# Layer 1, from the mixing sub-layer to the MLP: other tiles for the first weight group, no weight split on GpSimd, token-block sums from whole float32 tokens

## The chip, the core and the metric

The kernel runs on one core of a Trainium2 chip. Its engines have instruction streams of their own: TensorE (PE) multiplies and transposes, VectorE (DVE) and ScalarE (ACT) do elementwise work, GpSimd (POOL) does some of it too, SyncE (SP) issues nearly all DMAs. The metric is the device time of one execution in microseconds (us). Three runs of the kernel before took 1518.51, 1513.12 and 1522.53 us.

## The reference

Two layers over 512 latent tokens and 256 context tokens, 1024 features, all in float32. What matters here is the end of a layer's mixing and its MLP:

```
y   = merge_heads(attn, sgu, four, g_mix, w_out)        # output projection
x   = x + g1 * rmsnorm(y, g_post_mix)
hx2 = rmsnorm(x, g_pre_ff) * (1.0 + sc2) + sh2          # modulated tokens
x   = x + g2 * rmsnorm(square(relu(hx2 @ w_ff1)) @ w_ff2, g_post_ff)
```

In the second layer (layer 1, the last one) only the latent tokens go through this.

## The kernel before, in words

**Numbers.** Every operand of a product is held in two float32r parts, a high part (a cast) and a low part (the float32 value less the high part), and a product is three matmuls: high by high, high by low, low by high. So each weight block that comes in as `raw` is cast to `hi` by ACT (L234) and `lo` is made by a subtraction on DVE or POOL (L235, in `wunit`); each modulated token chunk is written in float32 by ACT (L393, `xv`), its high part by POOL (L395), its low part by DVE (L396).

**The MLP of layer 1.** The 4096 hidden features are worked in 16 groups of 256. Groups 0 and 1 use the plain product (`ff1`, L1106) for token blocks 0 and 1 and then for 2 and 3, since those tokens come in two halves. From group 2 on, `wino` (L1182) uses Winograd's form of Strassen's product: seven products in place of eight, which want sums of token blocks, S1 to S4 (`wino_a`), and differences of weights. With v11, v12 the modulated features of token blocks 0 and 1 (first and second half of the features) and v21, v22 those of blocks 2 and 3: S1 = v21 + v22, S2 = S1 - v11, S3 = v11 - v21, S4 = v12 - S2. Before, `wino_a` adds them up again from the two parts: per pair of feature chunks four adds on DVE and three on POOL for S1 to S3, then one on DVE and two on POOL for S4 (L956), and each S is split by ACT (L952) and DVE (L953). There are two such pairs.

**Tiles.** A tag of a pool is a ring: who asks for a tile of the tag waits until the one that had the buffer has been read for the last time. `w` has 8 tiles for weights, `raw` 4, `E` 4 and `PT` 2 belong to the attention while it runs, `Ma` 4; `h1`, `h2`, `h3` have two temporaries each. `h1` serves the sums s1 (and, in the new code, s3) and also the rectified hidden features `r` (L1122). The hidden products `h...` sit in two PSUM banks (tag S) until ACT has read them into `r`. The transposed tokens `xT` (L379) sit in two other banks.

**Order.** A scheduler places the instructions of each engine in one fixed order by a timeline of its own, with earlier calls of the program first. At run time an engine works strictly down its list. So what matters is which row stands ahead of which.

**Names.** In the rows `h100x` is layer 1, hidden group 0, half 0 of its 256 features, latent tokens; `h110x` the same of group 1. `raw_f`, `hi_f`, `lo_f` are weights of the MLP, `po1x` the output projection, `Ma1x` the split attention output, `at1x` the same before the split, `xr1x` the residual, `y1x` its normalised tokens, `f11x` the two parts of the modulated tokens, `wt`, `w` the products of Winograd's form, `f210x` the second product of the MLP for group 0.

Of the kernel before, what the change touches and what calls it, by code (L numbers as in the profile page):

```python
# [11 lines left out]
F32 = mybir.dt.float32  # L12
F32R = mybir.dt.float32r
BF16 = mybir.dt.bfloat16
AF = mybir.ActivationFunctionType
ALU = mybir.AluOpType
AX = mybir.AxisListType.X

P = 128
D = 1024  # L20
KD = D // P
# [10 lines left out]
# How far the first product of the MLP goes ahead of other work.  # L32
HP = 5
# The engine (v or p) that takes each of the two-operand steps of a hidden group: low parts of the weights of the
# first and second product, differences of weights, low parts of the hidden features.
# [10 lines left out]
# What the tensor engine does beside the attention units of a layer: U, G, F load the weights of a column group  # L46
# of the in-projection and u, g, f project a token block with them, fc, fx step through the Fourier mixing,
# gc, gx load the gates, oc, ox step through the output projection, ada through a modulation.
# [13 lines left out]
def _bc(ap, n, axis):  # L62
    """ap with a broadcast dimension of n put in at free position `axis`."""
    v = ap.unsqueeze(axis)
    shape = list(v.shape)
    shape[axis] = n
    return v.to_broadcast(shape)
# [3 lines left out]
def kernel(ctx: ExitStack, tc: tile.TileContext, a: dict, out: bass.AP):  # L71
# [15 lines left out]
    # Temporaries of a chain come from h1, h2, h3 in this order, so that chains never wait in a circle.  # L87
# [9 lines left out]
    # Streams that run side by side have tiles of their own; within a tag tiles are handed out in program order.  # L97
# [35 lines left out]
    # ------------------------------------------------------------- constants  # L133
# [18 lines left out]
    def rows_in(name, width, pairs):  # L152
        """Rows at given partitions of a zeroed [32, width] tile."""
        t = act.tile([32, width], F32, name=name, tag="slot")
        nc.gpsimd.memset(t, 0.0)
        for r0, src in pairs:
            nc.sync.dma_start(t[r0:r0 + src.shape[0], :], src)
        return t

    def turned(t, name, use):  # L160
        """Feature-major pieces of four chunks of such rows in PSUM, handed to `use`."""
# [7 lines left out]
    # silu(c), silu(c_ctx) as two columns of a zero-padded stationary operand  # L169
# [37 lines left out]
    # ---------------------------------------------------- common small helpers  # L207
# [4 lines left out]
    def power(o, i, scale, bias, expo):  # L212
        """o = (i * scale + bias) ** expo"""
# [11 lines left out]
    def wunit(src, shape, name, lo_eng=None, part=None, hi_pool=False):  # L225
        """A weight unit in two float32r parts whose sum is the float32 weight."""
# [11 lines left out]
    # ------------------------------------------------------------------ adaLN  # L238
    # modc[l]: feature-major columns for (sh1, sc1, sh2, sc2); gates go to DRAM rows.
# [7 lines left out]
    def ada_quad(l, q, alloc, alloct, wtile, side=None):  # L247
        """A sixth of the modulation of a layer. side: the rows of the weight times their entries are summed over
        the row chunks beside the tensor engine, which is left with the sum over the partitions."""
# [73 lines left out]
    def ada_rest(steps, alloc, alloct, side=None):  # L323
        """Steps through (layer, quad), one row chunk of the weight at a time."""
        for l, q in steps:
            yield from ada_quad(l, q, alloc, alloct, wa, side)
# [6 lines left out]
    # ------------------------------------------------- feature-major activations  # L333
    class Feat:
        """Feature-major tokens in two float32r parts, eight chunks of 128 features: with a tile for
        every chunk (whole=True, wide moving operands) or tiles for every token block."""
# [20 lines left out]
        def dests(self, k2, b0):  # L357
            """Destinations (hi, lo, slice of the [128, 2, 256] source) for chunks 2 k2, 2 k2 + 1."""
# [23 lines left out]
    def modulate(xns, feat, b0, l, which, alloc, order=range(KD // 2)):  # L382
        """Normalised token blocks b0, b0 + 1 -> modulated, feature-major, in two parts."""
# [4 lines left out]
        for k2 in order:  # L388
            ps = transposed(xns, nm, k2, alloc)
            v = h2([P, 2, n], F32, f"xv{nm}{k2}")  # L390
# [3 lines left out]
            for hi, lo, i in feat.dests(k2, b0):  # L394
                nc.gpsimd.tensor_scalar(out=hi, in0=v[:, i], scalar1=1.0, scalar2=1.0, op0=ALU.mult, op1=ALU.mult)  # L395
                nc.vector.tensor_tensor(out=lo, in0=v[:, i], in1=hi.bitcast(F32), op=ALU.subtract)  # L396

    # ------------------------------------------------------------- projections
# [14 lines left out]
    def in_group(l, nm, c0, c1, feats, consume, alloc, alloc2, units=None):  # L413
        """Loads a column group of w_in; the function returned projects one token block. What `consume` puts
        into `later` comes behind the products of the next block."""
# [19 lines left out]
    def rotate(ps, rope, nh, which, b, name):  # L435
        """Rotary embedding of a token-major [128, nh * 64] block in PSUM."""
# [14 lines left out]
    # ------------------------------------------------------------------ layers  # L451
    feats0 = {"c": Feat("c", "f00", False), "x": Feat("x", "f00", False)}
    # The start: shift and scale come a quarter of the features at a time, and behind each quarter the products
    # of its features with columns 256 .. 768 of the in-projection for the token blocks that are there.
# [8 lines left out]
    def ada_quarter(f):  # L463
        """Columns f * 256 .. of shift and scale of layer 0; four row chunks at a time share the tensor engine."""
# [46 lines left out]
    def layer(l, feats):  # L511
# [15 lines left out]
        # ---- in-projection and what follows from each column group  # L527
# [43 lines left out]
        def got_q(j, kind, b, ps, alloc):  # L571
            """Heads 4 j .. 4 j + 3: rotated, scaled, high parts over low parts along the partitions."""
# [24 lines left out]
        def gelu2(ps, out_, name):  # L597
            """out_ = 2 gelu(ps), in the tanh form; returns the [128, 256] temporary it used."""
# [60 lines left out]
        def part1(kind, k, hl, t0, n):  # L659
            """Tokens t0 .. t0 + n of a chunk of the gating and Fourier features."""  # L660
# [4 lines left out]
        def finish_s(kind, msf, nb):  # L665
            """msf: [128, nb], the mean squares of the Fourier part (plus eps) of every block."""
# [19 lines left out]
        def fourier(kind):  # L686
            """Three steps, for other work to lie between them."""
# [41 lines left out]
            for j in range(2):  # L729
                g = gg[j]  # L730
                # P in columns 0 .. H, then Q from its second column on
# [27 lines left out]
        def att_scores(kind, b, j):  # L759
            """Softmax numerators of four heads and 1 / their sums, token-major: (head, key chunk) -> [128, 128]."""  # L760
# [14 lines left out]
            for g in (0, 2):  # L775
                # negated scores, the masked ones 1e30, leave PSUM with their running minimum
# [32 lines left out]
        def att_values(kind, b, j, lob, pieces, ri, rest):  # L809
# [17 lines left out]
            # 1 / sum of every head and token, spread over the partitions of the head  # L827
# [37 lines left out]
        def postnorm(kind, b, y, G, which, dest, pieces=HALVES):  # L865
            """x + gate * rmsnorm(y), stored where the next reader wants it."""
# [23 lines left out]
        def out_proj(kind, alloc, alloc2):  # L890
            """Steps through the output projection: first the part of the gating and Fourier features, then for
            every two token blocks that of the attention and, at the end, what follows from it."""
# [35 lines left out]
            for b0 in bs[::2]:  # L928
# [7 lines left out]
                modulate(xns, f2[kind], b0, l, 1, alloc2)  # L936
# [5 lines left out]

        def wino_a(k2, alloc, which):
            """The sums S1 .. S4 of token blocks in Winograd's form of Strassen's product, for two feature chunks."""
# [40 lines left out]
        def flow(us, order, jobs):  # L985
            """Attention units, the scores of one ahead of the values of the one before. Behind every unit come
            the steps of `jobs` that `order` names; the attention goes first where both could."""
# [426 lines left out]
```

## Time and profile before

| what | value |
|---|---|
| runs | 1518.51, 1513.12, 1522.53 us; median 1518.51 us |
| profiled execution | span 1516.8 us from first to last instruction; the profile gives no other time for it |
| PE busy | 1429.4 us, 94% of the span |
| DVE, ACT, POOL busy | 74%, 49%, 42% |
| mean granted TensorE clock | 0.985 of full speed |
| DMA | 177.58 MB, 117 GB/s in the mean |

The span and the median of the runs differ by 1.7 us. PE is busy nearly always, so the time is PE's work and PE's idle time; but a matmul that runs at half clock counts as busy too. To find what a stage loses, one takes the stretches of 10 us: PE's busy time, the granted clock in the column PEclk, and then the instruction before which PE stood idle, with the releaser that the profile names.

### The profile page before, as it was taken

Reading aid. Unit: us, or ns where it says so; the run is one execution under the profiler, and the core shown is the slowest. Engines: PE = TensorE matmul, PEld = TensorE weight load, DVE = VectorE, ACT = ScalarE, POOL = GpSimd, SP = SyncE. Lnnn points to the kernel's source line nnn. Section 1 sums busy time; section 2 is a strip of 40 time slices with the busy share of each in tenths; the row PEclk is TensorE's granted clock in tenths of the full one; section 3 lists DMA queues with packets and bytes.
Section 4 is the critical chain, followed back from the end, with each engine's and each line's share of the span. In section 5 each row is a group of like instructions: output and inputs, shape, how many; then the busy total and the mean of one; then the engine's idle time right before and its main releaser. Section 6 shows DMA issues by size and latency. Waiting matters only on the chain. (4 is left out here: it accounts for less than half of the span.)

```text
span 1516.8 us, 24509 instructions
## 1 busy us (share of the span) xinstructions
PE 1429.4 (94%) x9133; PEld 1252.7 (83%) x9133; DVE 1115.8 (74%) x2003; ACT 747.7 (49%) x1673; POOL 644.3 (42%) x608
## 2 busy tenths in 40 slices
PE   7999999999899999999989998999998899999997
PEld 4688798788788878888878887998777788989886
DVE  3366887858687877878777758788757987777685
ACT  3346666556534333343333445476656555554452
POOL 3212636646634333334433546234346644344241
PEclk9999999999999999999999999999998999999999
DMA  9634322435132332325554344213134133223322
GB/s 328 228 122 154 112 74 84 137 115 167 42 100 84 124 111 84 126 70 174 167 172 129 125 160 139 72 55 87 39 100 165 56 112 111 93 89 100 110 84 84
DMA packets 94352, 177.58 MB, mean 117 GB/s; under 512 B 5796, under 2 KB 59524, under 8 KB 94232
## 3 DMA queue, kind: packets, MB, share of 16 engines
q1 hardware_dynamic: 91224, 170.93, 35.0%
q0 software_dynamic: 3008, 5.08, 1.2%
q8 instruction: 72, 1.18, 0.3%
q14 instruction: 48, 0.39, 0.1%
HBM read 166.62 MB, written 9.46 MB: 116 GB/s over the span
## 5 line engine op out<-in xcount | busy, mean ns | idle before, releaser
L1152 POOL TENSOR_TENSOR raw_f<-raw_f,raw_f 128x512 f32<-128x512 f32 x70 | 98.2, 1402 | 107.8 <-DVE raw_f L1152 89.5
L1147 ACT CAST Wf<-raw_f 128x512 fp32r<-128x512 f32 x98 | 60.4, 619 | 118.6 <-DMA raw_f<-in_w_ff 108.4
L266 DVE SCALAR_TENSOR_TENSOR acc<-wa,silu,acc 128x1024 f32<-128x1024 f32 x70 | 96.1, 1391 | 21.7 <-DMA wa<-in_w_ada 21.6
L1148 POOL TENSOR_TENSOR Wf<-raw_f,Wf 128x512 fp32r<-128x512 f32 x28 | 40.1, 1433 | 153.3 <-ACT Wf L1147 153.3
L1195 PE MATMUL wc<-f01c,Wf 128*128 128x256 f32 x672 | 98.5, 286 | 3.4 <-DVE p L1201 3.4
L1195 PEld LDWEIGHTS wc<-f01c,Wf 128*128 128x128 f32 x672 | 91.6, 194 | 7.9 <-DVE p L1201 3.8
L1148 DVE TENSOR_TENSOR Wf<-raw_f,Wf 128x512 fp32r<-128x512 f32 x70 | 62.0, 887 | 41.0 <-ACT Wf L1147 40.9
L234 ACT CAST hi_f<-raw_f 128x1024 fp32r<-128x1024 f32 x72 | 73.8, 1043 | 34.8 <-PE f208c L1247 6.6
L235 POOL TENSOR_TENSOR lo_f<-raw_f,hi_f 128x1024 fp32r<-128x1024 f32 x20 | 54.7, 2735 | 77.7 <-ACT hi_f L234 57.6
L1125 DVE TENSOR_TENSOR hx<-r,hx 128x256 fp32r<-128x256 f32 x98 | 61.5, 630 | 31.2 <-ACT r L1124 31.1
L235 DVE TENSOR_TENSOR lo_f<-raw_f,hi_f 128x1024 fp32r<-128x1024 f32 x52 | 76.6, 1478 | 1.3 <-ACT hi_f L234 1.0
L1123 ACT ACTIVATE hx<-r 128x256 fp32r<-128x256 f32 x112 | 45.4, 413 | 44.4 <-PE f203x L1247 8.7
L1182 PE MATMUL w<-f11x,Wf 128*128 128x256 f32 x336 | 65.1, 283 | 0.0
L1182 PE MATMUL w<-S,Wf 128*128 128x256 f32 x336 | 63.0, 283 | 0.0
L1122 ACT ACTIVATE r<-c 128x256 f32<-128x256 f32 x84 | 34.7, 414 | 55.5 <-DVE c L1201 43.4
L1182 PEld LDWEIGHTS w<-f11x,Wf 128*128 128x128 f32 x336 | 54.7, 191 | 1.5
L1182 PEld LDWEIGHTS w<-S,Wf 128*128 128x128 f32 x336 | 53.0, 191 | 1.7 <-issue 0.4
L1182 PE MATMUL w<-f01x,Wf 128*128 128x256 f32 x336 | 50.4, 284 | 1.9 <-ACT Wf L1147 1.0
L1182 PEld LDWEIGHTS w<-f01x,Wf 128*128 128x128 f32 x336 | 46.4, 191 | 5.3 <-ACT Wf L1147 1.4
L1124 ACT ACTIVATE r<-r 128x256 f32<-128x256 f32 x112 | 45.5, 413 | 1.9
L393 ACT ACTIVATE xvx<-xTx,mod 128x256 f32<-128x256 f32 x64 | 31.6, 560 | 18.2 <-PE xTx L379 11.9
L797 ACT ACTIVATE E0x<-E0x,mx_0x 128x512 f32<-128x512 f32 (+1 forms) x32 | 24.9, 778 | 12.9 <-DVE mx_0x L791 12.7
(1243 smaller groups left out, 4886.1 us busy)
## 6 DMA issues: line engine op xcount, KB each, us to landing
raw_f<-in_w_ff SPq DMA_DIRECT2D x128, 512.0 KB
wa<-in_w_ada SPq DMA_DIRECT2D x80, 512.0 KB
wq<-in_w_ada SPq DMA_DIRECT2D x16, 512.0 KB
raw_out0c<-in_w_out SPq DMA_DIRECT2D x8, 512.0 KB
raw_out0x<-in_w_out SPq DMA_DIRECT2D x8, 512.0 KB
res0x<-xr0x SPq DMA_DIRECT2D x8, 512.0 KB
raw_out1x<-in_w_out SPq DMA_DIRECT2D x8, 512.0 KB
xl0x<-in_x SPq DMA_DIRECT2D x4, 512.0 KB
```

The lines of the kernel that those rows point to most:

```text
L234: nc.scalar.copy(hi, raw)
L235: (lo_eng or nc.vector).tensor_tensor(out=lo, in0=raw, in1=hi.bitcast(F32), op=ALU.subtract)
L266: nc.vector.scalar_tensor_tensor(out=acc[r], in0=w, scalar=s, in1=acc[r], op0=ALU.mult, op1=ALU.add)
L1122: nc.scalar.activation(r, src, AF.Relu)
L1123: nc.scalar.activation(hv[:, 0], r, AF.Square)
L1124: nc.scalar.activation(r, r, AF.Square)
L1125: next(lo_h).tensor_tensor(out=hv[:, 1], in0=r, in1=hv[:, 0].bitcast(F32), op=ALU.subtract)
L1147: nc.scalar.copy(t[:, 0], src)
L1148: next(lo).tensor_tensor(out=t[:, 1], in0=src, in1=t[:, 0].bitcast(F32), op=ALU.subtract)
L1152: next(diff).tensor_tensor(out=o, in0=x, in1=y, op=ALU.subtract)
L1182: nc.tensor.matmul(ps, W[w][:, wl, k], A[k // 2][:, k % 2, xh], start=(m == 0), stop=(m == 11))
L1195: nc.tensor.matmul(ps, W[f"{k // 4 + 1}{j + 1}"][:, wl, k % 4], f2["c"].ap(k, xh, 0, CTX), start=(m == 0), stop=(m == 3 * KD - 1))
```

## The change

Only layer 1 is touched (`last` in the code); layer 0 and all that comes before the last output projection stay as they are.

1. Hidden group 0: the split weights go to tiles of `PT` and `E`, which the attention has left, in place of `w`. Group 1's hidden features go to `w` in place of `E`.
2. The low parts of these weights are all made on DVE; before, the second half of each group was made on POOL.
3. `modulate` of the latent tokens goes through the feature chunk pairs in the order 0, 2, 1, 3 and keeps the float32 values of token blocks 0 and 1 in two slots (`vw`). For blocks 2 and 3 (`vl`) the sums S1 to S4 are made right there, from the float32 values: per pair three adds on DVE and one on POOL. `wino_a` is not called any more in this layer.

```diff
-    def modulate(xns, feat, b0, l, which, alloc, order=range(KD // 2)):
+    def modulate(xns, feat, b0, l, which, alloc, order=range(KD // 2), keep=None, after=None):
...
-            v = h2([P, 2, n], F32, f"xv{nm}{k2}")
+            v = keep(k2) if keep else h2([P, 2, n], F32, f"xv{nm}{k2}")
...
+            if after:
+                after(k2, v)
...
-                modulate(xns, f2[kind], b0, l, 1, alloc2)
+                if last:
+                    modulate(xns, f2[kind], b0, l, 1, alloc2, (0, 2, 1, 3), *(wino_keep if b0 == 0 else wino_sums))
+                else:
+                    modulate(xns, f2[kind], b0, l, 1, alloc2)
...
+        def keep_whole(k2):
+            if k2 % 2 == 0:
+                for k in (0, 2):
+                    if ("t", k) not in whole:
+                        whole["t", k] = slot([P, 2, 2, 2 * P], F32, f"vw{k}")
+            whole[0, k2] = whole["t", k2 // 2 * 2][:, k2 % 2]
+            return whole[0, k2]
+
+        def keep_last(k2):
+            whole[1, k2] = h2([P, 2, 2 * P], F32, f"vl{k2}")
+            return whole[1, k2]
+
+        def sums_at(k2, v):
+            if k2 < 2:
+                return
+            k2 -= 2
+            v11, v12, v21, v22 = (whole[i, k2 + j] for i in range(2) for j in (0, 2))
+
+            def part(i, f):
+                t = slot([P, 2, 2, 2 * P], F32R, f"S{l}{i}{k2}")
+                WS[i, k2] = t
+                nc.scalar.copy(t[:, :, 0], f)
+                nc.vector.tensor_tensor(out=t[:, :, 1], in0=f, in1=t[:, :, 0].bitcast(F32), op=ALU.subtract)
+
+            def made(al, i, x, y, op, eng=nc.vector):
+                t = al([P, 2, 2 * P], F32, f"s{i}{l}{k2}")
+                eng.tensor_tensor(out=t, in0=x, in1=y, op=op)
+                return t
+
+            s1 = made(h1, 1, v21, v22, ALU.add)
+            s2 = made(h3, 2, s1, v11, ALU.subtract)
+            part(1, s1)
+            part(2, s2)
+            part(3, made(h1, 3, v11, v21, ALU.subtract, nc.gpsimd))
+            part(4, made(h3, 4, v12, s2, ALU.subtract))
...
-                           .rearrange("(k p) f -> p k f", p=P), [P, 4, 256], f"f1{l}{g}{u}", nc.gpsimd if g < 2 and u else None) for u in range(2)]
+                           .rearrange("(k p) f -> p k f", p=P), [P, 4, 256], f"f1{l}{g}{u}",
+                           nc.gpsimd if u and not last else None, (ptile, etile)[u] if last and g == 0 else None)
+                     for u in range(2)]
...
-            H[g]["x"] = [etile([P, 2, SEQ], F32R, f"hx{l}{g}{j}") for j in range(2)]
+            H[g]["x"] = [(wtile if last and g else etile)([P, 2, SEQ], F32R, f"hx{l}{g}{j}") for j in range(2)]
...
-        for which in range(2):
+        for which in range(0 if last else 2):
```

How the rows move. First ACT, at the start of layer 1's MLP. Before, the rectified features `r100x` follow the last copies of the residual's chain, far ahead of the first S. Of the new list (`vl` are the float32 tokens of blocks 2 and 3, `S` the sums' high parts):

```order
L394 ACTIVATE vl_12612<-xTx_12607,mod_4141 128x256
L394 ACTIVATE vl_12622<-xTx_12617,mod_4141 128x256 [waits PE_49,Pool_49]
L974 CAST S_12594<-s_12589 128x2x256 [waits DVE_49]
L974 CAST S_12599<-s_12597 128x2x256
L974 CAST S_12604<-s_12602 128x2x256 [waits DVE_49]
L974 CAST S_12631<-s_12627 128x2x256 [waits DVE_49]
L974 CAST S_12634<-s_12629 128x2x256 [waits DVE_49]
L974 CAST S_12639<-s_12637 128x2x256 [waits Pool_49]
L1172 ACTIVATE r100x_12712<-h100x_12687 128x256 [waits DVE_49]
L1173 ACTIVATE hx_12659<-r100x_12712 128x256 [waits Activation_49]
```

`r100x`, which clears the PSUM bank of `h100x`, now stands behind seven of the eight S casts, and takes the `h1` tile that `s_12627` (S1 of the second pair) had.

PE at the same place, the new list: the transposes of token blocks 2 and 3 and the first product of hidden group 1.

```order
L379 MATMUL xTx_12607<-ident,y1x_12133 128x128 [waits PE_49,Activation_49]
L379 MATMUL xTx_12607<-ident,y1x_12148 128x128
L379 MATMUL xTx_12617<-ident,y1x_12133 128x128 [waits PE_49,Activation_49]
L379 MATMUL xTx_12617<-ident,y1x_12148 128x128
L1156 MATMUL h110x_12747<-f11x_12313,hi_f_12663 128x256 [waits Activation_49]
L1156 MATMUL h110x_12747<-f11x_12313,hi_f_12663 128x256
```

Before, `h110x` followed `h101x` at once, and these transposes came 35 to 70 rows later, between the products of group 1 and of the second half. Now nothing but transposes lies between `h101x` and `h110x`.

DVE at the end of the output projection, the list before:

```order
L914 SCALAR_TENSOR_TENSOR y1x_12133<-po1x_12479,ra_1x_12107,y1x_12133 128x512
L882 SCALAR_TENSOR_TENSOR xr1x_12401<-y1x_12011,rp_1x_12411,xr1x_12401 128x512
L656 SCALAR_TENSOR_TENSOR Ma1x_12126<-at1x_12221,cols,Ma1x_12126 128x128 x2
L235 TENSOR_TENSOR lo_f_12612<-raw_f_12609,hi_f_12611 128x1024
```

and the new one:

```order
L917 SCALAR_TENSOR_TENSOR y1x_12133<-po1x_12477,ra_1x_12107,y1x_12133 128x512
L885 SCALAR_TENSOR_TENSOR xr1x_12401<-y1x_12011,rp_1x_12411,xr1x_12401 128x512
L235 TENSOR_TENSOR lo_f_12664<-raw_f_12661,hi_f_12663 128x1024
L885 SCALAR_TENSOR_TENSOR xr1x_12401<-y1x_12011,rp_1x_12411,xr1x_12401 128x512
L235 TENSOR_TENSOR lo_f_12670<-raw_f_12667,hi_f_12669 128x1024
L659 SCALAR_TENSOR_TENSOR Ma1x_12126<-at1x_12221,cols,Ma1x_12126 128x128 x2
```

All six weight splits of groups 0 and 1 and of the second product now stand on DVE ahead of the low part of the last attention unit (`Ma1x` from `at1x_12221`, L656, now L659); before, none of them did.

## Rows read from the trace of the kernel before

**Rows 1.** Stretches: length, busy PE, PEld, DVE, ACT, POOL (count), PEclk, DMA share, GB/s.
```profile
1140.00:1150.00 10.00, 6.35 (x29) 5.55 (x29) 10.00 (x11) 7.42 (x13) 8.12 (x8) 0.66 0.63 215
...
1190.00:1200.00 10.00, 4.94 (x20) 3.89 (x19) 9.96 (x10) 5.64 (x9) 7.05 (x5) 0.75 0.00 0
1200.00:1210.00 10.00, 10.00 (x64) 9.31 (x64) 10.00 (x15) 3.75 (x8) 3.78 (x3) 0.91 0.35 107
```
**Rows 2.** Timeline of PE: start, length, line, tiles, idle before and releaser.
```profile
1136.40 0.62 PE L909 MATMUL po1x<-hi_out1x,Ma1x 128*128 128x512 f32 x2
1137.92 0.38 PE L851 MATMUL ar1x<-unit,at1x 128*128 128x1 f32 x2 [0.89 <-POOL at1x L847]
...
1141.29 1.75 PE L379 MATMUL xTx<-ident,y1x 128*128 128x128 f32 x7 [2.82 <-DVE y1x L370]
...
1151.02 0.58 PE L1106 MATMUL h100x<-f11x,hi_f 128*128 128x256 f32 x1 [3.12 <-DVE f11x L396]
...
1156.98 0.50 PE L1106 MATMUL h110x<-f11x,hi_f 128*128 128x256 f32 x2
...
1168.16 0.60 PE L379 MATMUL xTx<-ident,y1x 128*128 128x128 f32 x4
...
1189.88 0.28 PE L1182 MATMUL wt<-S,Wf112t 128*128 128x256 f32 x1
1191.41 0.39 PE L1182 MATMUL wt<-S,Wf112t 128*128 128x256 f32 x1 [1.25 <-ACT S L952]
1194.72 1.40 PE L1182 MATMUL wt<-S,Wf112t 128*128 128x256 f32 x6 [2.92 <-DVE S L953]
1197.01 1.44 PE L1182 MATMUL wt<-S,Wf112t 128*128 128x256 f32 x5 [0.89 <-DVE S L953]
...
1201.87 0.41 PE L1247 MATMUL f211x<-hi_f,hx 128*128 128x512 f32 x1
```
**Rows 3.** Timeline of DVE in the same form.
```profile
1122.43 0.75 DVE L914 SCALAR_TENSOR_TENSOR y1x<-po1x,ra_1x,y1x 128x512 f32<-128x512 f32 x1 [1.75 <-PE po1x L909]
...
1134.52 0.61 DVE L656 SCALAR_TENSOR_TENSOR Ma1x<-at1x,cols,Ma1x 128x128 fp32r<-128x128 f32 x2
...
1138.40 2.83 DVE L370 TENSOR_SCALAR y1x<-xr1x,r_pre1mx 128x1024 f32<-128x1024 f32 x1 [1.12 <-POOL r_pre1mx L217]
...
1146.55 3.40 DVE L235 TENSOR_TENSOR lo_f<-raw_f,hi_f 128x1024 fp32r<-128x1024 f32 x1
...
1150.89 1.21 DVE L235 TENSOR_TENSOR lo_f<-raw_f,hi_f 128x1024 fp32r<-128x1024 f32 x1
...
1159.37 0.74 DVE L370 TENSOR_SCALAR y1x<-xr1x,r_pre1mx 128x1024 f32<-128x1024 f32 x1
...
1172.17 1.29 DVE L1148 TENSOR_TENSOR Wf<-raw_f,Wf 128x512 fp32r<-128x512 f32 x2
...
1187.72 6.34 DVE L956 TENSOR_TENSOR s<-s,f11x 128x512 f32<-128x512 f32 x5
```
**Rows 4.** Timeline of ACT in the same form.
```profile
1146.23 1.05 ACT L234 CAST hi_f<-raw_f 128x1024 fp32r<-128x1024 f32 x1 [0.19 <-DMA raw_f<-in_w_ff]
...
1156.55 0.38 ACT L1122 ACTIVATE r100x<-h100x 128x256 f32<-128x256 f32 x1 [3.86 <-PE h100x L1106]
...
1168.24 1.93 ACT L393 ACTIVATE xvx<-xTx,mod 128x256 f32<-128x256 f32 x4 [1.47 <-PE xTx L379]
```
**Rows 5.** Timeline of POOL in the same form.
```profile
1138.34 2.34 POOL L235 TENSOR_TENSOR lo_f<-raw_f,hi_f 128x1024 fp32r<-128x1024 f32 x1
...
1165.67 0.92 POOL L395 TENSOR_SCALAR f11x<-xvx 128x512 fp32r<-128x512 f32 x1 [0.28 <-ACT xvx L393]
1166.56 1.28 POOL L956 TENSOR_TENSOR s<-f11x 128x512 f32<-128x512 f32 x1
```
**Rows 6.** DMA issues on SP: start, length, line, tile.
```profile
1117.95 0.37 SPq L228 DMA_DIRECT2D raw_f<-in_w_ff  x1
...
1141.74 1.66 SPq L228 DMA_DIRECT2D raw_f<-in_w_ff  x2
```

More of the change, by code (lines that the diff above doesn't have):

```diff
@@ L941, in layer @@
         WS = {}
+        whole = {}
+        def keep_whole(k2):
[28 more added lines that the diff above has]
+            part(4, made(h3, 4, v12, s2, ALU.subtract))
+        wino_keep, wino_sums = (keep_whole,), (keep_last, sums_at)
         def wino_a(k2, alloc, which):
@@ L1265, in gtile @@
             return wp.tile(shape, dt, name=name, tag="gate", bufs=1)
-        SA = [(slot, slot)] * 4 if last else [(slot, slot), (gtile, ptile), (etile, etile), (slot, slot)]
+        SA = [(slot, slot), (gtile, ptile), (etile, etile), (slot, slot)]
         for t0 in (0, 2 * P):
```

## The prediction

> **What bounds the kernel now.** I read the page first: PE is busy 94% of the span, so an edit pays only by PE work that it removes or by PE time that is lost. The same matmuls are done before and after, so only lost time is at stake. Then I took PE in stretches of 10 us over the passage from mixing to MLP of layer 1. The reader sees two holes [rows 1]: in 1140 to 1150 PE is busy 6.35 of 10 at a granted clock of 0.66, in 1190 to 1200 it is busy 4.94 at 0.75; from 1200 on it is busy throughout. PE's timeline names the releasers [rows 2].
>
> - End of the output projection: `po1x` ends at 1137.0. PE waits 0.89 and 2.82 us, the second for `y1x` (L370). DVE's row shows why: that L370 took 2.83 us against 0.74 for its like [rows 3], beside a weight split of 2.34 on POOL [rows 5].
> - First product: 3.12 us for `f11x` (L396), which stood on DVE behind a split of 3.40, where one alone takes 1.21 [rows 3].
> - Winograd's sums: 1.25 + 2.92 + 0.89 = 5.06 us for S [rows 2]. DVE is busy 9.96 of 10 there [rows 1]; five adds took 6.34 us, 1.27 each, against 1.29 for two, 0.65 each, with POOL free [rows 3]. After this PE runs at half clock from 1194.72 to 1201.87: 7.15 us less the 0.89 idle, half of it lost, 3.1 us. Together 8.2 us.
>
> So there is something to win, some 12 us of idle and about 7 us of half clock. Whether it is won depends on what stands in its place.
>
> **The change part by part.**
>
> *The late S wait goes: -8.2 us.* Made during `modulate`, all sums are there some 15 us before the first `wt`, which before stood at 1189.88. Eight of ten POOL subtractions and four of eighteen DVE operations on sums and their splits disappear; that by itself is worth nothing on PE beyond these 8.2.
>
> *Weight splits, group 0 in PT and E.* The casts can start before the output projection has left its tiles, and PE would not wait for weights in any case: before, its waits are for tokens. But all six splits (four of the first product, two of the second) now stand on DVE, each 1.21, ahead of `Ma1x`, the last input of the output projection. One of them, of the second product, needs a third load, which has no `raw` buffer before 1117.95, when before the fourth issue was let go [rows 6]. A pair issued at 1141.74 reached its reader at 1146.23, which still waited 0.19 [rows 4, 6]: up to 4.5 us. So its cast begins near 1122.4, takes 1.05 and its split 1.21, and the DVE row that stood at 1122.43 (L914) comes at 1124.7, 2.3 later. Two more splits follow ahead of `at1x` and two more ahead of `Ma1x`: 4.8. That is 7.1 at most; DVE's waits for PE, such as the 1.75 ahead of L914, take up a part. I take 5.5: `Ma1x` low at 1140.0 for 1134.52 [rows 3], the output projection ends at 1142.5 for 1137.0. Bounds 3 and 7.
>
> *The first product.* The POOL splits that held DVE are gone. So L370 costs 0.74 for 2.83, and I put the transposes at 1144, 2.6 later than 1141.29. From there to `h110x` it took 15.7 us before (to 1156.98), of which about 3 for the held split. `h100x` and `h101x` end near 1156.7, as before: the loss at the projection's end and the gain behind it cancel.
>
> *A new wait at `h110x`.* This is the term that decides. `h110x` needs the PSUM bank of `h100x`, and ACT clears it with `r100x`. Before, ACT did so at 1156.55 and `h110x` followed at 1156.98 [rows 2, 4]. Now `r100x` stands behind seven S casts and uses the `h1` tile of the second s1, which is free when DVE has made its low part. Queued behind it on ACT are the other `r`; behind those, on PE, are `f210x` and `h111x`. The chain from the tokens of block 3:
>
> 1. They are normed (L370) at 1159.37 to 1160.1 before [rows 3]. Their chain starts 5.5 later, without splits of 3.40 and 1.21 in it and without casts on ACT: between 1156.5 and 1161. I take 1158; eight transposes, 0.9: 1158.9.
> 2. ACT writes four `vl`, 1.93 [rows 4]; POOL makes a high part, 0.92, then S3 of the first pair, 1.28, which holds DVE [rows 5]; DVE the low part, 0.65; only then the `h2` tile is free for four more `vl`, 1.93. Sum 6.7.
> 3. DVE does eight operations from the second s1 to its low part: 5.2 at 0.65 each, 10.1 at 1.27 each. One POOL subtraction falls among them: 5.2 + 1.3 = 6.5.
> 4. `r100x`, 0.38.
>
> So `h110x` starts at 1158.9 + 6.7 + 6.5 + 0.4 = 1172.5, 15.5 late. Meanwhile PE only has the transposes of blocks 2 and 3, which it needs not do later: 14 that stood behind 1156.98, at 0.60 for four at most, some 1.6 us. Net +13.9. A hole of over 10 us is longer than those of 3.12 and 2.92 in front of stretches at half clock, so I add between 0 and 3.1 (the last such stretch), 2.3.
>
> *Sum.* +15.5 - 1.6 + 2.3 - 8.2 = +8.0 on the span of 1516.8: 1524.8. The median of the runs lies 1.7 higher; I forecast **1525**. At best (normed at 1156.5, eight operations without any hold, clock kept) `h110x` starts at 1169.5: +12.5 - 1.6 - 8.2 = +2.7. At worst (1161, 1.27 each, 3.1 of clock) near 1179: +22 - 1.6 + 3.1 - 8.2 = +15.3. Own range 1518 to 1534.
>
> *The rest* costs nothing: hidden features of group 1 in `w` leave six tiles of `w` for group 2's seven operands, and PE then has over 30 us of plain products as cover; the late groups are as before, PE being busy 10.00 of 10. If that cover goes, the seventh operand's cast and split show once; by the full-width ones, 1.05 [rows 4] and 1.21 [rows 3], at most 2.3.
>
> **A rule against the rows.** The rows say that a DVE operation with two SBUF inputs hardly moves while POOL runs one: 3.40 for 1.21, beside a POOL split. The Trainium skill, page "SBUF — State Buffer", section "SBUF: two separate sides", goes further: the shared port pair of DVE and GpSimd is an exclusive lock, held for the whole instruction, and the other engine fully blocks. By that, the two splits and eight subtractions that leave POOL give DVE all their time back, and the change should be faster. The trace agrees with the lock; what it leaves open is whether DVE's time is PE's time here. That is the first rival.
>
> **The rivals.**
>
> *The lock was the whole loss (faster).* Two splits of about 2.34 and eight subtractions of about 1.28 [rows 5] leave POOL: 2 x 2.34 + 8 x 1.28 = 15 us of DVE's time. If the sums end before PE has run out of work, the 8.2 us go and no new hole opens; of the first part's 2.82 and 3.12 with their half clock another 3 to 4 go: 1516.8 - 12 = 1505, about 1506 in the median. For it: DVE's full stretch at 1190 to 1200. Against it: PE has 1.6 us of work as cover for a chain of 13.6. It decides if `r100x` starts by about 1161. Chance 0.18.
>
> *It cancels.* The sums hang on DVE's work in both places: 8.2 us lost late become 8 lost early, and the transposes save their bit: 1516 to 1519. For it: the lower ends above. It takes a normed block 3 by 1155 or a DVE without waits. Chance 0.15.
>
> *The weight load holds the projection (slower).* ACT works in order, so the cast of the second product's weights holds the `at1x` copies and norms behind it, and DVE's split the rest. Each us that this load lands after 1122.4 goes on to `Ma1x`, and no slack is left, since PE has nothing but `po1x` there; after 1126 the hole at the projection's end exceeds 8 us, brings its own half clock, and pushes block 3 by 4: 1524.8 + 4 + 3 + 3 = 1535, range 1531 to 1542. Against it: the pair issued at 1141.74, two loads on this queue together, cost its reader only 0.19 of waiting, and this load goes alone. Chance 0.12.
>
> **How the numbers follow.** Forecast 0.55, the rivals 0.18, 0.15 and 0.12. The range that leaves out 2 in 10 is 1508 to 1536: below, half of the first rival, above, most of the third. A difference of 1% (15 us) is about what a measurement of this kernel tells from no change. Faster by more: only the far end of the first rival, 0.06. Slower by more: the greater part of the third and the top of the forecast, 0.10. Within: 0.84.
>
> **What would show it.** In the new profile: `wt` without waits for S and no half clock near the first Winograd group; POOL subtractions on sums two in number; `po1x` ending near 1142 with waits for `Ma1x` of DVE or ACT; a wait of 10 us or more at `h110x`, releaser ACT (`r100x`), with DVE on L975 and L979 without a gap; half clock behind it. The forecast is wrong if `h110x` follows the transposes within 5 us, or if the output projection ends by 1138.

## The result

The changed kernel took 1528.13 us (median, 1525.73 to 1530.35), the kernel before beside it 1517.47 us (1513.12 to 1522.53). The ratio is 1.0070, interval 1.0053 to 1.0087: 10.7 us slower by the medians. The forecast was 1525 us: +8.0 on the span by its sum, +6.5 on the median of the first three runs. The change lies inside the 1% for which the prediction gave 0.84; but this measurement told 0.7% from no change, with an interval of 0.17% to each side, so the prediction's remark that 1% is about what can be told was too coarse.

The profiled span is 1526.4 us, 9.6 more than before. This is three differences, told apart by the start of the first `po1x`, of the first `f2110x` (hidden group 10, far behind the passage) and the end. Up to the first `po1x` (1082.86 us, before 1079.86) the new execution is 3.0 us late; nothing is changed there. From `po1x` to `f2110x` it takes 320.0 us in place of 309.7: +10.3, the change. Behind `f2110x` it is 3.7 us shorter: the profile of before has 3.9 us of waits for `Y1x` there (1.44, 0.44, 1.35, 0.35, 0.33), the new one 1.7 us of waits (1.41 for `hx`, 0.33 for `Y1x`), which is 2.2 of it; where the rest lies was not found. The middle difference agrees with the medians; against a second profile of the kernel before (e5 below) it is 8.7. Where places of two profiles are compared below, they are counted from the first `po1x`; the rows show the times of their own profile.

The stretches of 10 us in the new profile (columns as in [rows 1]):

```profile
1140.00:1150.00 10.00, 6.05 (x18) 4.06 (x18) 8.58 (x13) 3.88 (x10) 4.31 (x7) 0.66 0.77 229
1150.00:1160.00 10.00, 8.05 (x56) 6.79 (x57) 8.29 (x13) 6.42 (x15) 6.54 (x9) 1.00 0.59 211
1160.00:1170.00 10.00, 3.17 (x23) 2.25 (x21) 6.36 (x8) 4.99 (x12) 5.21 (x7) 0.78 0.25 89
1170.00:1180.00 10.00, 3.50 (x16) 3.50 (x17) 9.20 (x14) 5.58 (x13) 2.38 (x2) 0.50 0.00 0
...
1190.00:1200.00 10.00, 10.00 (x80) 9.74 (x79) 0.85 (x2) 3.60 (x9) 0.48 (x1) 1.00 0.01 2
```

The hole of 1190 to 1200 [rows 1] is gone; a larger one stands at 1160 to 1180, in whose second half DVE is at its fullest (9.20 of 10). PE's timeline (start, length, idle before and releaser):

```profile
1141.06 0.50 PE L912 MATMUL po1x<-hi_out1x,Ma1x 128*128 128x512 f32 x1 [3.59 <-ACT Ma1x L658]
...
1144.68 1.22 PE L912 MATMUL po1x<-hi_out1x,Ma1x 128*128 128x512 f32 x2 [2.06 <-DVE Ma1x L659]
...
1147.40 1.05 PE L912 MATMUL po1x<-hi_out1x,Ma1x 128*128 128x512 f32 x2
...
1160.71 0.28 PE L1156 MATMUL h101x<-f11x,lo_f 128*128 128x256 f32 x1
1161.79 0.87 PE L379 MATMUL xTx<-ident,y1x 128*128 128x128 f32 x6 [0.81 <-DVE y1x L370]
1163.45 0.66 PE L379 MATMUL xTx<-ident,y1x 128*128 128x128 f32 x4 [0.78 <-ACT vl L394]
1164.36 0.66 PE L379 MATMUL xTx<-ident,y1x 128*128 128x128 f32 x4 [0.26 <-ACT vl L394]
1176.50 0.80 PE L1156 MATMUL h110x<-f11x,hi_f 128*128 128x256 f32 x2 [11.48 <-ACT r100x L1172]
1177.09 0.41 PE L1156 MATMUL h110x<-f11x,lo_f 128*128 128x256 f32 x1
...
1182.64 0.40 PE L1156 MATMUL h111x<-f11x,hi_f 128*128 128x256 f32 x2
1182.88 0.28 PE L1156 MATMUL h111x<-f11x,lo_f 128*128 128x256 f32 x1
...
1210.43 1.12 PE L1232 MATMUL wt<-S,Wf112t 128*128 128x256 f32 x8
```

The reader sees three answers to [rows 2]. The output projection ends at 1148.45, with two new waits for `Ma1x`. `h110x`, which followed `h101x` at once, waits 11.48 us for ACT's `r100x`, and up to 1182.64 a matmul of 256 columns takes 0.41 where it takes 0.28 afterwards. And `wt` comes without any wait for S.

What ACT and then DVE do in front of `r100x`:

```profile
1126.91 1.05 ACT L234 CAST hi_f<-raw_f 128x1024 fp32r<-128x1024 f32 x1 [3.40 <-DMA raw_f<-in_w_ff]
...
1167.61 1.93 ACT L394 ACTIVATE vl<-xTx,mod 128x256 f32<-128x256 f32 x4 [1.12 <-DVE f11x L397]
1169.42 2.18 ACT L974 CAST S<-s 128x512 fp32r<-128x512 f32 x4
1174.86 1.14 ACT L974 CAST S<-s 128x512 fp32r<-128x512 f32 x2 [3.26 <-DVE s L979]
1176.06 0.38 ACT L1172 ACTIVATE r100x<-h100x 128x256 f32<-128x256 f32 x1
```
```profile
1128.00 1.23 DVE L235 TENSOR_TENSOR lo_f<-raw_f,hi_f 128x1024 fp32r<-128x1024 f32 x1 [3.66 <-ACT hi_f L234]
...
1138.07 0.74 DVE L370 TENSOR_SCALAR y1x<-xr1x,r_pre1mx 128x1024 f32<-128x1024 f32 x1
...
1141.35 1.22 DVE L235 TENSOR_TENSOR lo_f<-raw_f,hi_f 128x1024 fp32r<-128x1024 f32 x1
...
1143.14 1.22 DVE L235 TENSOR_TENSOR lo_f<-raw_f,hi_f 128x1024 fp32r<-128x1024 f32 x1
1144.28 0.61 DVE L659 SCALAR_TENSOR_TENSOR Ma1x<-at1x,cols,Ma1x 128x128 fp32r<-128x128 f32 x2
...
1169.58 0.76 DVE L979 TENSOR_TENSOR s<-vl,vl 128x512 f32<-128x512 f32 x1 [0.26 <-ACT vl L394]
...
1173.08 1.75 DVE L979 TENSOR_TENSOR s<-s,vw 128x512 f32<-128x512 f32 x1
1174.75 1.28 DVE L975 TENSOR_TENSOR S<-s,S 128x512 fp32r<-128x512 f32 x2
1175.95 0.68 DVE L979 TENSOR_TENSOR s<-vw,s 128x512 f32<-128x512 f32 x1
```

The second pair's `vl` ends at 1169.54 on ACT; DVE then works without a gap until the low parts at 1174.75 have freed the `h1` tile (they end at 1176.03); the last of ACT's S casts ahead of `r100x` ends at 1176.00; `r100x` follows at 1176.06. L370 is back at 0.74 (2.83 in [rows 3]): POOL has no split any more.

### The profile page after: what moved, and what is told of

It is laid out like the page before. It is cut to its first block, busy times and chain, and to the rows that moved or that the text cites. A ratio compares the mean times of both kernels' runs of the same rounds, so it can differ in the third digit from the quotient of the medians.

```text
span 1526.4 us, 24505 instructions
## 1 busy us (share of the span) xinstructions
PE 1428.5 (94%) x9133; PEld 1248.8 (82%) x9133; DVE 1111.0 (73%) x2001; ACT 749.1 (49%) x1673; POOL 626.3 (41%) x598
## 5 line engine op out<-in xcount | busy, mean ns | idle before, releaser
L235 DVE TENSOR_TENSOR lo_f<-raw_f,hi_f 128x1024 fp32r<-128x1024 f32 x54 | 81.6, 1517 | 8.6 <-ACT hi_f L234 8.5
L1175 DVE TENSOR_TENSOR hx<-r,hx 128x256 fp32r<-128x256 f32 x98 | 58.1, 597 | 38.5 <-ACT r L1174 38.4
L235 POOL TENSOR_TENSOR lo_f<-raw_f,hi_f 128x1024 fp32r<-128x1024 f32 x18 | 48.6, 2700 | 79.6 <-ACT hi_f L234 57.9
L800 ACT ACTIVATE E1x<-E1x,mx_1x 128x512 f32<-128x512 f32 (+1 forms) x32 | 24.9, 778 | 12.7 <-DVE mx_1x L794 12.5
```

The lines of the kernel that those rows point to most:

```text
L235: (lo_eng or nc.vector).tensor_tensor(out=lo, in0=raw, in1=hi.bitcast(F32), op=ALU.subtract)
L800: nc.scalar.activation(e, e, AF.Exp, bias=m, scale=-1.0, accum_out=su[:, h, 0:1])
L1175: next(lo_h).tensor_tensor(out=hv[:, 1], in0=r, in1=hv[:, 0].bitcast(F32), op=ALU.subtract)
```

## The experiments

The theory: the sums cost PE the wait at `h110x`, through the ring `h1` and the order on ACT, and give the late wait back; the weight tiles and splits only delay the projection. The rivals: the late projection is the whole loss; POOL's hold on DVE was the whole loss of before; there is simply too much DVE work. Each kernel ran beside the kernel before, whose median was 1517.47 us beside the change, 1519.74 beside e1 to e4, 1517.60 beside e5 to e8 and 1518.71 beside e9 and e10; kernels of different groups are better compared by the ratios. Times from the first `po1x`, in us, of one profile each (end of the last `po1x`, start of the first of the others). The order of PE's rows around `f211x` differs between the kernels, so `f2110x` is the column to compare with the ratios:

| kernel | `po1x` ends | `h110x` | `f211x` | `f2110x` | median us | ratio to before, 95% interval |
|---|---|---|---|---|---|---|
| before | 57.2 | 77.1 | 118.4 | 309.7 | | 1 |
| e5, before again | 57.2 | 78.2 | 119.5 | 311.3 | 1520.31 (one run) | |
| the change | 65.6 | 93.6 | 128.5 | 320.0 | 1528.13 | 1.0070 [1.0053, 1.0087] |
| e1, tiles and splits alone | 65.5 | 78.8 | 118.0 | 314.0 | 1523.01 | 1.0026 [1.0013, 1.0038] |
| e2, sums alone | 57.2 | 94.7 | 129.0 | 318.7 | 1529.36 | 1.0064 [1.0051, 1.0077] |
| e3, the change, own r | 65.6 | 78.6 | 113.8 | 304.1 | 1512.77 | 0.9961 [0.9947, 0.9975] |
| e4, sums, own r | 57.2 | 78.9 | 119.4 | 307.9 | 1516.78 | 0.9986 [0.9974, 0.9998] |
| e6, splits on DVE alone | 57.2 | 78.9 | 120.0 | 311.5 | 1518.66 | 1.0008 [0.9998, 1.0017] |
| e7, e4 with splits on DVE | 57.2 | 76.1 | 116.7 | 305.4 | 1512.23 | 0.9961 [0.9948, 0.9973] |
| e8, e3 with POOL splits | 62.0 | 79.3 | 123.8 | 312.6 | 1518.24 | 1.0004 [0.9991, 1.0016] |
| e9, e3 with own `vl` | 57.8 | 72.8 | 116.0 | 306.1 | 1512.63 | 0.9962 [0.9948, 0.9976] |
| e10, e7 with own `vl` | 57.2 | 82.0 | 116.8 | 306.4 | 1516.71 | 0.9991 [0.9977, 1.0005] |

**e1: parts 1 and 2 alone.** `wino_a` late and its S tiles as before:

```diff
-                if last:
-                    modulate(xns, f2[kind], b0, l, 1, alloc2, (0, 2, 1, 3), *(wino_keep if b0 == 0 else wino_sums))
-                else:
-                    modulate(xns, f2[kind], b0, l, 1, alloc2)
+                modulate(xns, f2[kind], b0, l, 1, alloc2)
...
-        SA = [(slot, slot), (gtile, ptile), (etile, etile), (slot, slot)]
+        SA = [(slot, slot)] * 4 if last else [(slot, slot), (gtile, ptile), (etile, etile), (slot, slot)]
...
-        for which in range(0 if last else 2):
+        for which in range(2):
```

> Parts 1 and 2 of the change alone (tiles of PT and E, all low parts of the weights on DVE); the sums are made late from the two parts, as before. Theory (the wait at h110x and the missing wait for S both belong to part 3; parts 1 and 2 only delay the end of the output projection and take POOL's splits away from DVE): the output projection ends 8 to 11 us later than before (1137.0), as it does in the changed kernel (1148.25), the held L370 and L397 win some 6 of it back, h110x follows h101x within 1 us, and the wait for S at the first wt stays, 4 to 6 us: 1521 us, 1518 to 1524. Rival A (the port lock was the whole loss, so splits off POOL pay): 1512 or less, no longer wait for Ma1x. Rival B (the late projection is the whole loss of the changed kernel): 1527 or more.

Measured: 1523.01 us, within the theory's range. The projection ends as late as in the changed kernel, yet `h110x` is only 1.7 us late (0.6 against e5). The late wait stayed, 5.56 us where it was 5.06. PE's row:

```profile
1201.14 1.44 PE L1229 MATMUL wt<-S,Wf112t 128*128 128x256 f32 x5 [5.56 <-DVE S L998]
```

So the late projection is not the loss of 10 us, and taking POOL's splits off DVE doesn't pay by itself. Rivals A and B fall.

**e2: part 3 alone.** `ff1_open` as before:

```diff
-                           nc.gpsimd if u and not last else None, (ptile, etile)[u] if last and g == 0 else None)
+                           nc.gpsimd if g < 2 and u else None)
...
-            H[g]["x"] = [(wtile if last and g else etile)([P, 2, SEQ], F32R, f"hx{l}{g}{j}") for j in range(2)]
+            H[g]["x"] = [etile([P, 2, SEQ], F32R, f"hx{l}{g}{j}") for j in range(2)]
```

> Part 3 alone (sums from the whole float32 tokens); weights of group 0 in w, their second halves split on POOL, hidden features of group 1 in E, as before. Theory (r100x stands behind seven S casts on ACT and needs the h1 tile of the second s1): the projection ends near 1137 as before, but PE waits 10 to 15 us at h110x for ACT's r100x, and has no wait for S later: h110x 17 to 19 us late, 8.2 + 1.6 of it given back: 1525 us, 1522 to 1529. Rival (the late end of the projection is what pushes block 3 and so the sums; without it the sums have their time): the wait at h110x is 5 us or less, and with the late wait gone 1510 to 1517.

Measured: the whole loss of the change (1529.36, just above the 1522 to 1529 named), without its tiles and with the projection ending as before. PE's and ACT's rows:

```profile
1136.80 0.38 PE L854 MATMUL ar1x<-unit,at1x 128*128 128x1 f32 x2 [0.87 <-POOL at1x L850]
...
1173.40 0.79 PE L1156 MATMUL h110x<-f11x,hi_f 128*128 128x256 f32 x2 [11.48 <-ACT r100x L1172]
```
```profile
1171.76 1.14 ACT L974 CAST S<-s 128x512 fp32r<-128x512 f32 x2 [3.25 <-DVE s L979]
1172.97 0.38 ACT L1172 ACTIVATE r100x<-h100x 128x256 f32<-128x256 f32 x1
```

The same 11.48 us: the wait belongs to the sums.

**e3: the change, with r out of `h1`.** A tile of `w` holds the four `r` of groups 0 and 1 for token blocks 0 and 1:

```diff
+            if last and g == 1:
+                H["r"] = wtile([P, 4, 256], F32, f"r{l}")
...
-            r = h1([P, n], F32, f"r{nm}")
+            r = H["r"][:, 2 * g + j] if last and g < 2 and t0 == 0 else h1([P, n], F32, f"r{nm}")
```

> The changed kernel, but the rectified features r of groups 0 and 1, token blocks 0 and 1, get a tile of w of their own in place of h1; nothing else. ACT's r100x then stands ahead of the S casts. Theory (the ring h1 ties h110x to the sums; this wait is the price of the change): h110x follows h101x within 2 us, the 11.48 us go, no late wait for S; left are the late end of the projection, some 4 us at h101x's end (1160.8 for 1156.98), and the gain of 8.2: 1513 us, 1509 to 1518. Rival (the sums are simply too much work for DVE and ACT at that place, wherever r stands: PE waits for f11x or hx in place of r): 1521 or more, with waits of 5 us or more behind h111x.

Measured as expected: 0.9961, 15.4 us better than the change itself by the medians (1528.13 and 1512.77), 1.1% by the ratios. The expectation's 4 us at the end of `h101x` compare absolute times; from the first `po1x`, `h110x` stands 1.5 us later than before. ACT clears the bank at once, and PE doesn't stop:

```profile
1162.80 0.38 ACT L1175 ACTIVATE r<-h100x 128x256 f32<-128x256 f32 x1 [0.36 <-PE h100x L1159]
```
```profile
1163.08 0.28 PE L1159 MATMUL h101x<-f11x,lo_f 128*128 128x256 f32 x1
1163.23 0.50 PE L1159 MATMUL h110x<-f11x,hi_f 128*128 128x256 f32 x2
```

The rival of too much DVE work falls: DVE does the same sums, PE finds other work beside them, and the waits that its timeline shows from `h110x` to `f2110x` are 0.73 us in all. What e3 does not separate is the ring from the order: with its own tile `r` also moved ahead of the S casts on ACT, and in the changed kernel the casts and the low part that frees the tile end within 0.03 us of each other.

**e4: part 3 alone, with r out of `h1`** (e2 with the edit of e3, the tile taken from `PT`).

> Part 3 alone, with r of groups 0 and 1, token blocks 0 and 1, in a tile of PT of its own. Neither the late projection nor the wait at h110x. Theory: both prices are gone and the 8.2 us of the late wait for S with its half clock are won: 1509 us, 1505 to 1513. Rival (DVE's work is only moved; the sums in the first half take from PE there what they gave later): 1515 to 1522, with waits of PE for f11x, vl or hx between 1157 and 1185 of 5 us or more.

Measured 1516.78, off by 8 us and at the rival's time, though PE's waits for `f11x` between 1157 and 1185 are 3.1 us, not the 5 named. What the theory left out are POOL's two splits, which this kernel has kept. DVE's and PE's rows (POOL's splits of 2.34 and 2.85 stand at 1140.63 and 1147.14):

```profile
1140.70 2.82 DVE L370 TENSOR_SCALAR y1x<-xr1x,r_pre1mx 128x1024 f32<-128x1024 f32 x1 [1.13 <-POOL r_pre1mx L217]
...
1147.70 2.84 DVE L397 TENSOR_TENSOR f11x<-vw,f11x 128x512 fp32r<-128x512 f32 x1
```
```profile
1155.38 0.58 PE L1159 MATMUL h100x<-f11x,hi_f 128*128 128x256 f32 x1 [1.85 <-DVE f11x L397]
1155.76 0.41 PE L1159 MATMUL h100x<-f11x,lo_f 128*128 128x256 f32 x1
...
1176.61 0.39 PE L1159 MATMUL h100x<-f11x,hi_f 128*128 128x256 f32 x1 [2.52 <-POOL f11x L396]
```

From the first `h100x` (63.9 from the first `po1x`; 68.7 in e3) to `h110x` it takes 15.0 us, 9.9 in e3, with matmuls of 0.41 as at half clock. The projection's early end is spent there; behind `h110x` the last row's wait and another of 0.62 follow.

**e5: the kernel before again**, unchanged.

> The kernel before once more, unchanged, to see how far two profiled executions of one program differ. Expected: span between 1513 and 1523 us; between the last transpose of the attention (pt1x) and h110x 38.7 us as in the first profile, to the first wt 71.6, to the first f211x 80.0, each within 1 us. If these distances move by several us, differences of a few us between the kernels' profiles say nothing.

Its stages lie up to 1.7 us from the first profile's, more than the 1 us expected: differences of that size in the table mean nothing.

**e6: the kernel before, splits on DVE**; **e7: e4 with the same edit.**

```diff
-                           ... nc.gpsimd if g < 2 and u else None)
+                           ... nc.gpsimd if g < 2 and u and not last else None)
```

> The kernel before with one edit: the low parts of the weights' second halves of groups 0 and 1 are made on DVE in place of POOL; tiles and late sums as before. Theory (a POOL split holds DVE for its length: L370 2.83 for 0.74, a split 3.40 for 1.21; these holds and the half clock behind them cost PE time, but two splits of 1.21 now stand on DVE): h110x comes 2 to 5 us earlier than in the kernel before, the late wait for S stays: 1516 us, 1513 to 1519. Rival (two more splits on DVE take what the holds gave): h110x within 1 us of before, 1518 to 1522.

> Part 3 with r in a tile of PT, as before in this study, but with all low parts of the weights on DVE; tiles of the weights as in the kernel before (1516.78 us with the POOL splits). Theory (what was missing there against the version with parts 1 and 2 is POOL's two splits, which hold DVE beside L370 and f11x and leave the first product at half clock): L370 takes 0.74 in place of 2.82, h100x to h110x takes 10 to 12 us in place of 15.0: 1512 us, 1508 to 1515. Rival (the early end of the output projection itself is worth nothing, and the DVE splits behind it hold f11x): 1516 to 1520.

e6 is the same as before, its rival: L370 takes 0.75 and `h100x` starts 2.3 us earlier, but `h110x` isn't earlier. The gain is lost inside the first product. The granted clock is 0.67 in 1140 to 1150 and 0.50 in 1150 to 1160; PE's busy time times the share of the clock that was not granted, in stretches of 5 us from 50 to 80 us behind the first `po1x`, makes 6.6 us, where the two profiles of before have 3.5 and 5.0 and e7 has 2.2. And PE waits 1.57 us for a high part that POOL makes late, behind an operation of one column that took 2.83 us, beside DVE's splits, where its like takes 0.19 with DVE idle:

```profile
1150.00:1160.00 10.00, 8.43 (x38) 7.89 (x38) 7.77 (x10) 4.36 (x12) 6.56 (x6) 0.50 0.83 275
```
```profile
1150.33 2.83 POOL L215 TENSOR_SCALAR r_pre1mx<-ms_pre1mx 128x1 f32<-128x1 f32 x1 [3.80 <-ACT junk_pre1mx L222]
...
1153.77 0.62 POOL L395 TENSOR_SCALAR f11x<-xvx 128x512 fp32r<-128x512 f32 x1
```
```profile
1154.44 0.58 PE L1106 MATMUL h100x<-f11x,hi_f 128*128 128x256 f32 x1 [1.57 <-POOL f11x L395]
```

e7 gains on e4 3.8 us by the ratios (0.9961 for 0.9986), 4.6 by the medians, as its theory said, though `h100x` to `h110x` takes 13.3 us, more than the 10 to 12 named:

```profile
1140.76 0.75 DVE L370 TENSOR_SCALAR y1x<-xr1x,r_pre1mx 128x1024 f32<-128x1024 f32 x1 [1.12 <-POOL r_pre1mx L217]
```

So taking POOL's splits away paid in the version with early sums and not in the kernel before. Why is not shown: in e6 the gain is gone before `h110x`, ahead of the late wait for S, so that wait did not absorb it.

**e8: e3 with the second halves' splits back on POOL.**

> The changed kernel with r in a tile of w of its own (1512.77 us), and the low parts of the second halves of groups 0 and 1 back on POOL; the tiles of the change stay. Four splits stand on DVE ahead of the last Ma1x in place of six, the late weight load stays ahead of them. Theory (the two splits between xr1x and Ma1x, 1.22 each, and the load's 3.4 of waiting both hold the projection): it ends 23 to 25 us behind the last transpose of the attention in place of 26.2, and POOL's splits hold DVE again: 1513 us, 1510 to 1517. Rival A (the load alone sets the end): it ends 26 us behind, and the time is 1514 or more. Rival B (only the number of splits on DVE sets it): 21 to 22 us, 1510 or less.

The projection ends 23.3 us behind the last transpose, as the theory said, but the gain of e3 is gone: 1518.24 us, outside the theory's range. Of the rivals neither fits: A's time does, its 26 us does not, and B has both wrong. One POOL split of 2.36 now stands beside the residual's chain, and PE waits behind it:

```profile
1137.06 3.88 DVE L885 SCALAR_TENSOR_TENSOR xr1x<-y1x,rp_1x,xr1x 128x512 f32<-128x512 f32 x2
```
```profile
1145.55 1.54 PE L379 MATMUL xTx<-ident,y1x 128*128 128x128 f32 x6 [3.29 <-DVE y1x L370]
```

PE's order also has the first `wt` much earlier here (99.2 from the first `po1x`, 112.0 in e3), so it waits for S again, 1.32 us. Up to `h110x` (79.3, in e3 78.6) only 0.7 us of the loss has come; most of it lies behind, where PE waits 0.88, 0.94 and 1.04 us for `f11x`, 1.32 for S and 0.88 for `Y1x`, and e3 has one wait of 0.47. What part of these the splits cause and what part the order wasn't separated.

**e9: e3 with the second pair of `vl` in a tile of `Ma`; e10: e7 with that pair in a tile of `PT`.** The edit of e9 (e10 has `ptile` for `mtile`):

```diff
-            whole[1, k2] = h2([P, 2, 2 * P], F32, f"vl{k2}")
+            if k2 % 2 == 0:
+                whole[1, k2] = h2([P, 2, 2 * P], F32, f"vl{k2}")
+            else:
+                if k2 == 1:
+                    whole["l"] = mtile([P, 2, 2, 2 * P], F32, "vl")
+                whole[1, k2] = whole["l"][:, k2 // 2]
```

> The changed kernel with r in a tile of w of its own (1512.77 us), and the second pair of vl in a tile of Ma of its own in place of h2. The ring Ma thereby hands out the tiles of the second product's weights of group 0 later, so their casts and splits stand behind the projection's end on ACT and DVE, among the sums; and only two splits stay ahead of the last Ma1x. Theory (these splits and their late load are what holds the projection, and its holes, 3.60 and 1.55 with half clock, are a loss of their own): it ends 19 to 21 us behind the last transpose of the attention in place of 26.2, h110x comes at 33 to 37 in place of 39.1: 1508 us, 1504 to 1511. Rival (the splits only move: f210x or the first product waits for them or for f11x behind them, 5 us or more): 1512 to 1518.

> Part 3 with r in a tile of PT and all low parts of the weights on DVE (1512.23 us), and the second pair of vl in a tile of PT of its own in place of h2. Theory (the second pair of vl waits for h2, that is for the sums of the first pair, and behind it f11x of token blocks 2 and 3 and PE, 2.64 and 0.62 us, with half clock after): these waits fall below 1 us: 1509 us, 1506 to 1511. Rival (DVE's chain of sums and low parts sets the pace of f11x there, whatever tile vl has): PE still waits 2 us or more for f11x of blocks 2 and 3: 1511 to 1514.

In e9 the projection ends at 57.8 and `h110x` comes 5.8 us earlier than in e3, as the theory said. It is taken back behind that, at the rival's time: at the second product's weights, whose splits now stand among the sums, PE waits 2.69 us (the rival named 5 or more), and matmuls at half clock around it cost some 2.6 us more, by the granted clock in stretches of 5 us:

```profile
1167.81 0.80 PE L1305 MATMUL f210x<-lo_f,hx 128*128 128x512 f32 x1 [2.69 <-DVE lo_f L235]
```

The median is that of e3. In e10 the waits for `f11x` of blocks 2 and 3 are gone, but the transposes of blocks 2 and 3 now stand ahead of `h110x` on PE and wait for block 3:

```profile
1160.20 0.87 PE L379 MATMUL xTx<-ident,y1x 128*128 128x128 f32 x6 [1.83 <-DVE y1x L370]
...
1163.96 0.80 PE L1164 MATMUL h110x<-f11x,hi_f 128*128 128x256 f32 x2
```

`h110x` comes 5.9 us later than in e7 by that, but by `f211x` the two are level again (116.8 and 116.7), and `f2110x` differs by 1.0. The profiled execution, 1514.25 us, is the fastest of e10's twelve; so where the 4.5 us between its median and e7's lie is not shown. The median is above both the theory's range and the rival's; neither had the order in it.

## Why the prediction was right

The forecast case came, and each step is found in its place. Against the first `po1x`, forecast and measured:

- **The late S wait:** gone, as said (-8.2); two POOL subtractions on sums are left.
- **The projection's end:** forecast +5.5, measured +8.4 (65.6 for 57.2), outside the bounds of 3 and 7. This is the term that was too small. The late load's cast stood 44.0 us behind the first `po1x` in place of the 42.5 that I took, and the two splits of 1.22 close ahead of L659 were counted against DVE's waits for PE, which didn't take them up. The third rival named this load, so its mechanism was there in part: the holes of 3.59 and 2.06 and the clock of 0.66. But its price was wrong. e1 has the same late end, and its `h110x` is 1.7 us late, 0.6 against e5: what the end loses, L370 and `f11x` without POOL's holds and a first product at full clock give back. That cancelling was forecast, but its sizes came right by luck in part: from the projection's end to the normed block 3 the forecast has 15.5 us, the profile 13.3, and this error takes back most of the 2.9 us by which the end was mis-sized.
- **The wait at `h110x`:** forecast 1172.5, that is 92.6 from the first `po1x`; measured 93.6. The chain's parts: `vl` of the second pair ends 6.9 us behind the transposes of 1162.66 (6.7 forecast); from there to `r100x` 6.5 (6.5 forecast); 0.38. e3 shows that it is this chain: with r out of `h1`, and so ahead of the casts, the wait is gone, while the projection ends as late (65.6) and the sums are still made in the first half (the last add starts at 97.0, the first `wt` at 112.0).
- **The clock:** from 1176.50 to 1182.64 at half, 3.1 us lost; 2.3 were taken, 3.1 was the bound.
- **The sum:** 16.5 + 3.1 - 1.6 - 8.2 = 9.8, against +10.3 in the profile and 10.7 in the medians. The 1.6 and the 8.2 are the forecast's own, not measured apart. Two slips in the prediction change nothing here: its best case adds up to 1169.7, not 1169.5, and +2.7 with the 1.7 of the median makes 1521, so the 1518 of its own range has no working.

The first rival (the lock was the whole loss) had the right observation: L370 and the splits got their time back. The Trainium skill's rule of an exclusive lock, "SBUF — State Buffer", section "SBUF: two separate sides", agrees with the rows here too: beside POOL's S3 of 1.57 from 1172.70, DVE's sum at 1173.08 took 1.75, and its like at 1175.95 0.68:

```profile
1172.70 1.57 POOL L979 TENSOR_TENSOR s<-vw,vl 128x512 f32<-128x512 f32 x1 [1.89 <-DVE S L975]
```

By that rule alone the change should have won, and e7 against e4 shows a win, 3.8 to 4.6 us, once the tie through `h1` is cut. In the change itself it went into the new hole; by e6, in the kernel before, it is worth nothing.

What stays open: what causes e1's 0.26%, of which its profile shows waits of PE behind `f211x`'s start (1.02 us for a weight's low part, 2.1 for `Y1x`), whether the ring or the order on ACT alone would hold `r100x` as long, why e3, e7 and e9, which lose their time in different places, come out alike at 1512 to 1513 us, what share of e8's loss is the split and what the order, and where e10's lies. A version with both e9's early projection and e3's early weights wasn't tried.

## What to carry over

Work moved to an earlier place on an in-order engine must be followed to the tiles that it borrows: here a temporary of 2 KB per partition, shared by the sums and the rectified features, tied the release of a PSUM bank, through that tile and the order on ACT, to the whole chain of sums, and giving the latter a tile turned 0.7% slower into 0.4% faster. Ask of each wait that a change removes what PE does at the new place; DVE's time saved became PE's time in one version (e7 against e4) and not in another (e6 against before), where PE's clock and a late POOL operation took it back. A late input at a stage's end may cost little if the next stage has as much to win: of 8.3 us in e1, 0.6 to 1.7 were left at `h110x`.

## What was not expected of the hardware

The hold seems to work the other way too. In e6 an operation of one column on POOL took 2.83 us for 0.19, above. In the changed kernel POOL's factors of one column per partition, two small operations each, took 0.55 us (L217) where DVE was idle as they began, and 1.74 beside DVE's split of 1.21 and addition of 0.74; L877 took 0.79 and 1.58. Spans on POOL are rough, but the starts of the two rows from 1135.56 lie 1.84 apart as well:

```profile
1130.74 0.79 POOL L877 TENSOR_SCALAR rp_1x<-ms_post1x,ms_post1x 128x1 f32<-128x1 f32 x1 [9.95 <-ACT junk_post1x L222]
...
1135.56 1.74 POOL L217 TENSOR_TENSOR r_pre1mx<-r_pre1mx,nhalf 128x1 f32<-128x1 f32 x1
1137.40 1.58 POOL L877 TENSOR_SCALAR rp_1x<-ms_post1x,ms_post1x 128x1 f32<-128x1 f32 x1
...
1160.40 0.55 POOL L217 TENSOR_TENSOR r_pre1mx<-r_pre1mx,nhalf 128x1 f32<-128x1 f32 x1
```

These factors stand in the chain of `xr1x` and `y1x`, which PE waits for at block 3; the prediction had them at no extra cost. For block 3 itself that held here: its factor is the last row, 0.55. The Trainium skill's rule named above states that either engine blocks the other; it was applied to DVE alone. No run took this apart.
